# A recorder that writes the static order of a hybrid diffusion layer: another price list for TensorE, and a rule on the share of large products

## The chip, the cores and the metric

The kernel runs on one core of a Trainium2 chip. The core has five engines with queues of their own: TensorE (PE in the profile, its weight loads PEld), VectorE (DVE), ScalarE (ACT), GpSimd (POOL) and SyncE (SP, which issues the DMAs here). Each takes its instructions in the order in which the program lists them and waits on semaphores for what the others deliver. The metric is the device time of the whole kernel in microseconds, the median over runs.

## The reference, cut to what matters

Two trunk layers over 1152 tokens (128 of a prompt, 1024 of a sample), model width 1024, all in float32:

```
h      = rms_norm(x) * (1 + scale) + shift                    # adaLN
parts  = split(h @ w_in)                                      # one wide projection
o_a    = softmax(q k^T) v            * silu(gate_a)           # 8 heads, latent K and V
o_b    = b_in * conv3(c_in * x_in)   * silu(gate_b)
o_c    = rms_norm(delta_fwd(q,k,v) + delta_bwd(q,k,v)) * silu(z)
m      = s_a*(o_a @ w_pa) + s_b*(o_b @ w_pb) + s_c*(o_c @ w_pc)   # s = sigmoid(parts)
x      = x + gate * (m @ w_o)
```

`delta_*` is a gated DeltaNet in chunks of 64 tokens, 8 heads of 64 by 64, one pass forwards and one backwards. Inside a chunk a unit triangular system is solved; from chunk to chunk a state goes on, so that each chunk needs the one before:

```
v_new = u - w @ S
o     = (q*exp(g)) @ S + attn @ v_new
S     = S * exp(g_last) + k_dec^T @ v_new
```

## The kernel before

Tokens lie in three blocks of 384 columns (`CH`), features on the 128 partitions. A large float32 product is made of three products of a high and a low part (`mm3s`), each 128 by 128 by 384. The layer has three stages: the front (all of `w_in` but the merge gates, and the DeltaNet), attention, and the mix (merge gates, branch projections, output projection).

In the front the projection is one stream of work, `ip`: per tile of weights and block of tokens 24 products into one PSUM tile, which the streams `ev` and `cv` take out. Beside it run the streams of the DeltaNet, for four pairs of heads and the prompt (5 jobs): `ga` (norms `kq`, decay `sg`, Gram products `G`), `gv`, `gb` (the triangular solve of 32 by 32 blocks on DVE and POOL, 31 steps), `gz` (the products `pw` of 32 by 32 blocks), `gc` (the chain from chunk to chunk) and `gd` (the outputs `oi`, `oa`). A step of `gc` is: four calls `p` (64 by 64, into PSUM), DVE takes them out in one operation over both directions and then adds the values in two, one per direction (`scr`), four calls `pv`, DVE again, four calls `pk`, and two DVE operations, one per direction, that make the new state (`SH`). There are 16 such steps per pair of heads. A call on 64 by 64 float32 operands stands in the trace as two PE instructions: a group of four calls as x8.

The order in which every engine gets these instructions is written out while the program is built, by a list scheduler: class `Flow`. Each stream is a Python generator that yields one recorded instruction (`Op`) at a time. The front and the mix are made so; attention has an order by hand. `Flow` keeps a model clock: `free[e]` is when engine `e` is through with what it has, `ready(op)` is when the operands are there (ends of the operations that wrote them plus `LAG` between the two engines). `run` (L230) looks at the head of each stream, and takes the one that can start first, by

```
best = min(cand, key=lambda x: (x[0] + 0.02 * x[1], x[1]))
```

where x[0] is the start and x[1] the stream's rank (`RK`: gc 3; gb 6; gz, gv, gd 4; ga 7; ip 9). So a stream of rank 3 goes ahead of `ip` when it can start up to 0.12 us later. A further loop lets a lower rank in when its wait is short. `put` (L190) then moves the model's clock by the operation's cost and hands the instruction on.

The cost of a PE call comes from `Eng.cost` (L115). A product with at most 64 rows costs its number of weight columns over 600, or over 1200 where it writes to partitions other than 0: a call on 64 by 64 costs 0.107 or 0.053 us, on 32 by 32 0.053 or 0.027 us. A float32r product of 256 columns or more costs its columns over 2400 (0.160 us for 384). A float32 product of two columns (`kq`) costs 0.003 us. A DVE `tensor_tensor` costs 0.065 us and its elements over 960, `scalar_tensor_tensor` 0.131 us and the same.

All recorded instructions bear the line of the recorder that calls them (L98; those of attention and those called through other lines L95), so the rows below are told apart by the names of the tiles.

Of the kernel before, what the change touches and what calls it, by code (L numbers as in the profile page):

```python
# [39 lines left out]


class Op:
    __slots__ = ("e", "f", "r", "w", "c", "m")


class Wait:
# [9 lines left out]
def _span(ap):  # L56
    dims = ap.ap
    if ap.space == DRAM:
        lo, p0, p1 = ap.offset, 0, 1
        rest = dims  # L60
    else:
        ps, pn = dims[0]
        p0, lo = ap.offset // ps, ap.offset % ps
        p1 = p0 + pn
        rest = dims[1:]
    hi = lo + 1
    for s, n in rest:
        if s > 0:
            hi += s * (n - 1)
        else:  # L70
            lo += s * (n - 1)
    return p0, p1, lo, hi


def _free(ap):
    n = 1
    for _, k in ap.ap[1:]:
        n *= k
    return n


class Eng:
# [7 lines left out]
    def __getattr__(self, m):  # L90
        real = getattr(self.real, m)

        def call(*a, **kw):
            if not self.k.rec:
                return real(*a, **kw)  # L95
            op = Op()
            op.e = self.e
            op.f = lambda: real(*a, **kw)  # L98
            aps = [x for x in a if hasattr(x, "tensor")]
            out = kw.get("out")  # L100
            outs = [out] if out is not None else [aps.pop(0)]
            if kw.get("accum_out") is not None:
                outs.append(kw["accum_out"])
            ins = aps + [v for n, v in kw.items() if n not in ("out", "accum_out") and hasattr(v, "tensor")]
            if m == "matmul" and not kw.get("start", True):
                ins.append(outs[0])
            op.w = [(self.k.key(x), _span(x)) for x in outs]
            op.r = [(self.k.key(x), _span(x)) for x in ins]
            op.c = self.cost(m, outs[0], ins, kw)
            op.m = ins[0].ap[-1][1] / 1200.0 if self.e == "PE" else 0.0  # L110
            return op

        return call

    def cost(self, m, out, ins, kw):  # L115
        n = max([_free(out)] + [_free(x) for x in ins if x.space != DRAM]) if self.e != "PE" else _free(out)
        if self.e == "PE":
            if m == "transpose":
                return n * 2 / 2400.0
            r = ins[1].dtype == F32R  # L120
            t = n * ((1 if n >= 256 else 4) if r else 4) / 2400.0
            if ins[0].ap[0][1] <= 64:
                t = ins[0].ap[-1][1] / (1200.0 if out.offset // out.ap[0][0] else 600.0)
            return t
        if self.e == "DVE":
            return (0.131 if m == "scalar_tensor_tensor" else 0.065) + n / (160.0 if m == "reciprocal" else 960.0)
        if self.e == "ACT":
            return (0.307 if ins and ins[0].space != PSUM and n > 256 else 0.13) + n / 1600.0
        if self.e == "POOL":
            if kw.get("op") == ALU.pow:  # L130
                return 0.15 + n * 0.175
            return (0.15 if m != "tensor_tensor" else 0.1) + n / (1200.0 if m != "tensor_tensor" else 475.0)
        run = 1 << 30
        for x in [out] + ins:
            c = 1
            for st, k in reversed(x.ap[0 if x.space == DRAM else 1:]):
                if st != c:
                    break
                c *= k
            run = min(run, c)  # L140
        return out.nbytes() / 360e3 * (2 if run < 128 else 1)


class Flow:
# [8 lines left out]
    def __init__(self, k):  # L153
# [3 lines left out]
        self.ev = set()  # L157
        self.pace = {}

    def ready(self, op):  # L160
        t = 0.0
        for lst, wr in ((op.r, False), (op.w, True)):
            for key, (p0, p1, lo, hi) in lst:
                ps = key[0] == "P"
                for q0, q1, l2, h2, end, eng, w in self.log.get(key, ()):
                    if eng != op.e and ps:

                        hit = (q0 // 32 < -(-p1 // 32) and p0 // 32 < -(-q1 // 32) and l2 // 512 <= (hi - 1) // 512
                               and lo // 512 <= (h2 - 1) // 512)
                    else:  # L170
                        hit = (w or wr) and q0 < p1 and p0 < q1 and l2 < hi and lo < h2
                    if hit:
                        end += self.LAG[eng, op.e]
                        if end > t:
                            t = end
        return t

    def note(self, op, end):
        for lst, w in ((op.r, False), (op.w, True)):
            for key, sp in lst:  # L180
# [5 lines left out]
                if len(recs) > 96:  # L186
                    recs.sort(key=lambda x: x[4])
                    del recs[:32]

    def put(self, op, s):  # L190
        f = self.free
        if op.e == "SP":
            f["SP"] = s + 0.06
            hw = max(s, f.get("HW", 0.0))
            f["HW"] = hw + 0.45
            d = max(hw + 1.1, f.get("DMA", 0.0))
            f["DMA"] = d + op.c
            self.note(op, d + op.c)
        else:
            if op.e == "PE":  # L200
                s = max(s, f.get("PEW", 0.0) + op.m)
                f["PEW"] = s
            f[op.e] = s + op.c
            self.note(op, s + op.c)
        op.f()

    def step(self, st):
# [22 lines left out]
    def run(self, streams, until=None, evs=()):  # L230

        for n, s in streams.items():
            if "head" not in s:
                s.update(head=None, end=False, wait=None)
        names = sorted(streams, key=lambda n: streams[n]["rank"])
        while True:
            moved = True
            while moved:
                k0 = len(self.ev)
                for n in names:  # L240
                    self.step(streams[n])
                moved = len(self.ev) != k0
            if all(streams[n]["end"] for n in (names if until is None else until)) and all(e in self.ev for e in evs):
                return
            cand = []
            for n in names:
                op = streams[n]["head"]
                if op is not None:
                    cand.append((max(self.free.get(op.e, 0.0), self.ready(op)), streams[n]["rank"], n, op))
            if not cand:  # L250
                raise RuntimeError("streams wait for each other: %s" % {n: streams[n]["wait"] for n in names})
            best = min(cand, key=lambda x: (x[0] + 0.02 * x[1], x[1]))
            for x in cand:
                if x[3].e == best[3].e and x[1] < best[1]:
                    wait = x[0] - best[0]
                    if wait <= 0 or wait < self.WIN and wait < self.PREF * (best[3].c - wait):
                        best = x
                        break
            streams[best[2]]["head"] = None
            self.put(best[3], best[0])  # L260
# [9 lines left out]
class Kern:  # L270
# [618 lines left out]
    def conv_put(self, c, put):  # L889
        RA, RB = self.cbuf["RA"], self.cbuf["RB"]  # L890
        if c == 0:
            yield put(RA[:, 1:129], 0, 128)
            yield put(RA[:, 131:387], 128, 384)
        elif c == 1:
            yield put(RA[:, 387:580], 0, 193)
            yield put(RB[:, 0:193], 191, 384)
        else:
            yield put(RB[:, 193:577], 0, 384)
# [1652 lines left out]
```

## Time and profile before

| | |
|---|---|
| median of 3 runs | 3540.32 us (3534.69 to 3552.49) |
| the profiled execution | 3544.98 us, span 3543.2 us |
| PE busy | 3375.9 us (95%), 24654 products |
| DVE, POOL, ACT busy | 2310.6, 1538.9, 1187.1 us |
| mean granted TensorE clock | 0.97 |

By stage the span goes: front of layer 0 until about 975 us, attention until 1260, mix until 1800, then the same for layer 1 (front until 2700, attention until 2990, mix until the end). The DeltaNet's chain runs from about 300 to 850 us and from 2050 to 2590 us; these two stretches are called the mixed phases below. Busy PE means that a product is anywhere in the array: products overlap, so a time per product is best read from the start of one run of products to the start of the next.

### The profile page before, as it was taken

What the parts mean: (1) busy time and instruction counts of PE and PEld (TensorE: products, weight loads), DVE (VectorE), ACT (ScalarE), POOL (GpSimd) and SP (SyncE); (2) the same over time, 40 slices, a digit from 0 to 9 for tenths busy, and PEclk for the clock granted to TensorE, in tenths of its full rate; (3) what the DMA queues carried; (4) which work ended last, traced back from release to release, by engine and by line L of the source; (5) the groups of instructions that cost most, each with busy time, mean ns of one, the idle gap of its engine ahead of it and who ended that gap; (6) DMA issues with size and microseconds to landing.
All of it is one profiled execution on the core that took longest, in us unless ns stands there. A gap on an engine that the chain in (4) does not pass through costs nothing. (4 is left out here: it accounts for less than half of the span.)

```text
span 3543.2 us, 65525 instructions
## 1 busy us (share of the span) xinstructions
PE 3375.9 (95%) x24654; PEld 2903.7 (82%) x24654; DVE 2310.6 (65%) x5052; ACT 1187.1 (34%) x2551; POOL 1538.9 (43%) x1550
## 2 busy tenths in 40 slices
PE   7999999999899999999999999999998999999998
PEld 4988777778765699999999877777788658999998
DVE  4467776774566488856664777786455665833755
ACT  4432222223334333332444232122242443333233
POOL 3156546533157544424212645654322774444231
PEclk9999899999999999999999989999999999999999
DMA  5333213213733235466333223122256322434842
GB/s 190 98 100 77 55 54 83 59 57 122 230 83 79 51 110 162 145 203 195 123 103 107 74 75 83 47 57 73 71 187 188 73 64 70 135 100 129 256 143 87
DMA packets 381339, 389.64 MB, mean 110 GB/s; under 512 B 162016, under 2 KB 310176, under 8 KB 380640
## 3 DMA queue, kind: packets, MB, share of 16 engines
q1 hardware_dynamic: 381024, 385.46, 36.5%
q8 instruction: 195, 3.19, 0.4%
q14 instruction: 120, 0.98, 0.1%
HBM read 264.54 MB, written 120.72 MB: 109 GB/s over the span
## 5 line engine op out<-in xcount | busy, mean ns | idle before, releaser
L98 PE MATMUL ip<-h,wh_wi 128*128 128x384 f32 x5328 | 1170.5, 358 | 3.6 <-DVE gb L98 1.1
L98 PEld LDWEIGHTS ip<-h,wh_wi 128*128 128x128 f32 x5328 | 932.8, 194 | 60.1 <-issue 16.4
L95 POOL TENSOR_TENSOR acc<-acc,P 128x512 f32<-128x512 f32 x224 | 289.1, 1291 | 126.1 <-ACT P L95 110.1
L98 POOL TENSOR_TENSOR tmp<-M,X 128x2 f32<-128x2 f32 (+30 forms) x310 | 218.6, 705 | 283.4 <-DVE X L98 263.1
L95 DVE TENSOR_REDUCE mx<-s 128x1 f32<-128x384 f32 (+1 forms) x400 | 209.2, 544 | 163.9 <-PE s L95 154.5
L95 ACT ACTIVATE P<-st 128x512 f32<-128x512 f32 x292 | 173.5, 598 | 264.9 <-PE st L95 229.3
L95 PE MATMUL st<-q,K 97*128 97x512 f32 (+1 forms) x912 | 257.2, 393 | 0.0
L98 POOL TENSOR_TENSOR sl<-ss,sl 128x512 fp32r<-128x512 f32 x100 | 144.3, 1444 | 245.7 <-ACT sl L98 227.6
L98 POOL TENSOR_TENSOR wh_wi<-wri,wh_wi 128x512 fp32r<-128x512 f32 x112 | 151.9, 1366 | 155.4 <-ACT wh_wi L98 151.6
L98 PE MATMUL pp<-ob,wp 128*128 128x384 f32 x1152 | 204.1, 336 | 2.2 <-DVE ob L98 1.8
L98 DVE TENSOR_REDUCE X<-tmp 128x1 f32<-128x2 f32 (+30 forms) x620 | 184.6, 319 | 31.4 <-POOL tmp L98 23.6
L98 PEld LDWEIGHTS pp<-ob,wp 128*128 128x128 f32 x1152 | 199.1, 188 | 6.6 <-POOL ob L98 3.7
L98 PE MATMUL wop<-h,wh_wo 128*128 128x384 f32 x1152 | 202.9, 335 | 0.0
L98 PE MATMUL sg<-h,sl 128*128 128x288 f32 x1440 | 201.1, 296 | 0.1
L98 PEld LDWEIGHTS wop<-h,wh_wo 128*128 128x128 f32 x1152 | 199.7, 188 | 1.1
L98 PEld LDWEIGHTS sg<-h,sl 128*128 128x128 f32 x1440 | 194.4, 188 | 0.3 <-POOL sl L98 0.3
L98 POOL TENSOR_TENSOR mU<-mU,mt 128x384 f32<-128x384 f32 x96 | 112.6, 1173 | 182.0 <-DVE mt L98 182.0
L98 ACT ACTIVATE VT<-pv,sst 128x64 f32<-128x64 f32 x256 | 66.7, 311 | 365.4 <-DVE scr L98 349.1
L95 PEld LDWEIGHTS st<-q,K 97*128 97x128 f32 x912 | 164.0, 190 | 28.3 <-issue 11.5
L98 POOL TENSOR_TENSOR gm<-g,cst 128x256 fp32r<-128x256 f32 x144 | 107.1, 754 | 162.0 <-PE sg L98 126.3
L98 DVE TENSOR_TENSOR tmp<-M,X 128x2 f32<-128x2 f32 (+30 forms) x310 | 162.5, 524 | 18.3 <-POOL M L98 12.5
L98 DVE SCALAR_TENSOR_TENSOR ada<-wada,cs,ada 128x256 f32<-128x256 f32 x224 | 148.9, 703 | 23.2 <-DMA wada<-in_w_ada 20.7
(339 smaller groups left out, 6327.4 us busy)
## 6 DMA issues: line engine op xcount, KB each, us to landing
wri<-in_w_in SPq DMA_DIRECT2D x160, 256.0 KB, 3.4
mt<-mD SPq DMA_DIRECT2D x144, 192.0 KB, 2.9
wada<-in_w_ada SPq DMA_DIRECT2D x128, 128.0 KB, 2.3
wrp<-in_w_p SPq DMA_DIRECT2D x48, 256.0 KB, 3.6
mD<-C SPq DMA_DIRECT2D x80, 144.0 KB, 1.9
mD<-cu SPq DMA_DIRECT2D x80, 144.0 KB, 1.8
ss<-in_w_in SPq DMA_DIRECT2D x40, 256.0 KB, 4.0
ws<-in_w_in SPq DMA_DIRECT2D x40, 256.0 KB, 4.3
```

The source lines that it names most:

```text
L95: return real(*a, **kw)
L98: op.f = lambda: real(*a, **kw)
```

## The change

Only the recorder changes; each call to an engine stays as it was, and so do the operands. A PE operation gets `u` (rows, weight columns, output columns). `load` gives for it the share of the array's work (rows by weight columns over the whole array, times columns over 2400), a time (columns over 2400 plus 0.013 us from 256 columns on; 0.03 us up to 32 columns; 0.08 us for products that don't fill the array; 0.112 us else) and whether it fills the array. `product` replaces the cost in the model's clock by this time, adds 0.1 us where the product before was of the other kind, doubles it where the interval before held too little of the array's work, and keeps a list of recent products. `low` says of a small product that starts on another output than the last whether the recent work of the array, with its own, is under 0.46 of the recorder's own interval. In `run`, when the chosen operation is such a product, the first large PE product among the heads that can start within 0.1 us goes first.

```diff
@@ Eng.__getattr__: call
             op.m = ins[0].ap[-1][1] / 1200.0 if self.e == "PE" else 0.0
+            if self.e == "PE":
+                op.u = (ins[0].ap[0][1], ins[0].ap[-1][1], _free(outs[0]))
@@ Flow.__init__
+        self.win, self.part, self.last = {}, False, None
@@ Flow
+    GRID = 3.41
+    SLOW = 0.35
+    LOW = 0.46
+    SWITCH = 0.1
+    NEAR = 0.1
+    @staticmethod
+    def load(op):
+        k, m, n = op.u
+        part = k < 128 or m < 128
+        return k * m / 16384.0 * n / 2400.0, n / 2400.0 + 0.013 if n >= 256 else 0.03 if n <= 32 else 0.08 if part else 0.112, part
+    def low(self, op, s):
+        u, t, part = self.load(op)
+        if t > 0.15 or op.w[0][0] == self.last:
+            return False
+        return u + sum(x for e, x in self.recent if e > s + t - self.GRID) < self.LOW * self.GRID
+    recent = ()
+    def product(self, op, s):
+        u, t, part = self.load(op)
+        t = max(t, op.c) if t > 0.15 else t
+        if part != self.part:
+            t += self.SWITCH
+        self.part, self.last = part, op.w[0][0]
+        w = int(s / self.GRID)
+        if w > 1 and self.win.get(w - 1, 0.0) < self.SLOW * self.GRID:
+            t *= 2
+        self.win[w] = self.win.get(w, 0.0) + u
+        self.recent = [x for x in self.recent if x[0] > s - self.GRID] + [(s + t, u)]
+        return s + t
@@ Flow.put
             if op.e == "PE":
                 s = max(s, f.get("PEW", 0.0) + op.m)
                 f["PEW"] = s
-            f[op.e] = s + op.c
-            self.note(op, s + op.c)
+                f["PE"] = self.product(op, s)
+                self.note(op, f["PE"])
+            else:
+                f[op.e] = s + op.c
+                self.note(op, s + op.c)
@@ Flow.run
+            if self.LOW and best[3].e == "PE" and self.low(best[3], best[0]):
+                for x in cand:
+                    if x[3].e == "PE" and x[0] <= best[0] + self.NEAR and self.load(x[3])[1] > 0.15:
                         best = x
                         break
```

## Rows read from the trace of the kernel before

**Rows 1.** The page: its first line, and TensorE's clock in 40 slices.
```profile
span 3543.2 us, 65525 instructions
PEclk9999899999999999999999989999999999999999
```
**Rows 2.** Busy time by stretch: stretch, us, PE, PEld, DVE, ACT, POOL, clock, DMA, GB/s.
```profile
300.00:850.00 550.00, 526.76 (x5570) 414.11 (x5569) 377.02 (x1120) 139.86 (x395) 275.02 (x340) 0.93 0.26 68
2050.00:2590.00 540.00, 511.27 (x5521) 400.97 (x5520) 376.07 (x1105) 141.32 (x400) 266.00 (x336) 0.95 0.25 68
1260.00:1800.00 540.00, 527.00 (x3423) 521.46 (x3422) 397.42 (x658) 190.79 (x368) 198.48 (x153) 0.99 0.49 156
```
**Rows 3.** Groups by form, PE, first the whole span, then 300 to 850 us.
```profile
L98 PE MATMUL pp<-ob,wp 128*128 128x384 f32 x1152 | 204.1, 336 | 2.2 <-DVE ob L98 1.8
...
L98 PE MATMUL ip<-h,wh_wi 128*128 128x384 f32 x1486 | 361.6, 370 | 1.1 <-DVE gb L98 1.1
L98 PE MATMUL pv<-scr,ZT 64*64 64x64 f32 x576 | 48.5, 242 | 8.0 <-DVE scr L98 7.3
```
**Rows 4.** Timeline of PE at full clock: start, us, what, count.
```profile
501.56 0.34 PE L98 MATMUL pk<-scr,kt 64*64 64x64 f32 x8
501.84 0.79 PE L98 MATMUL ip<-h,wh_wi 128*128 128x384 f32 x3
502.60 0.30 PE L98 MATMUL p<-SH,kTb 64*64 64x64 f32 x2
...
503.46 0.38 PE L98 MATMUL sg<-gm,mr 128*128 128x256 f32 x1
...
504.86 0.30 PE L98 MATMUL pv<-scr,ZT 64*64 64x64 f32 x2
...
505.84 0.39 PE L98 MATMUL sg<-gm,mr 128*128 128x256 f32 x1
```
**Rows 5.** Timeline of PE in a stretch at half clock.
```profile
392.55 0.49 PE L98 MATMUL pk<-scr,kt 64*64 64x64 f32 x8
392.97 1.33 PE L98 MATMUL ip<-h,wh_wi 128*128 128x384 f32 x3
394.23 0.47 PE L98 MATMUL p<-SH,kTb 64*64 64x64 f32 x2
```
**Rows 6.** Busy time by stretch, as Rows 2, of that stretch.
```profile
383.00:414.00 31.00, 31.00 (x215) 22.59 (x216) 15.45 (x40) 4.53 (x15) 10.91 (x15) 0.51 0.06 20
```
**Rows 7.** Timeline of PE at full clock, groups that were not split.
```profile
519.76 0.34 PE L98 MATMUL p<-SH,kTb 64*64 64x64 f32 x8 [0.92 <-DVE SH L98]
520.04 0.62 PE L98 MATMUL ip<-h,wh_wi 128*128 128x384 f32 x2
...
521.55 0.82 PE L98 MATMUL pv<-scr,ZT 64*64 64x64 f32 x8
522.29 0.44 PE L98 MATMUL ip<-h,wh_wi 128*128 128x384 f32 x1
```
**Rows 8.** Timeline of PE: first and last pv and p split into 2 and 6.
```profile
347.24 0.47 PE L98 MATMUL pv<-scr,ZT 64*64 64x64 f32 x2
...
358.35 0.30 PE L98 MATMUL p<-SH,kTb 64*64 64x64 f32 x2
...
2466.71 0.47 PE L98 MATMUL p<-SH,kTb 64*64 64x64 f32 x2
...
2517.09 0.32 PE L98 MATMUL pv<-scr,ZT 64*64 64x64 f32 x2
```
**Rows 9.** Timeline of PE: products with two columns.
```profile
491.18 3.57 PE L98 MATMUL kq<-hm,P 128*128 128x2 f32 x16
```
**Rows 10.** Timeline of PE: first and last place where groups of two tiles stand together.
```profile
369.70 0.32 PE L98 MATMUL G<-kqT 64*64 64x128 f32 x1
...
2515.34 0.27 PE L98 MATMUL oa<-VT,at 64*64 64x64 f32 x2
```
**Rows 11.** Groups by form, DVE, 300 to 850 us.
```profile
L98 DVE TENSOR_TENSOR scr<-scr,vT 64x128 f32<-64x128 f32 x128 | 53.6, 419 | 3.6
L98 DVE SCALAR_TENSOR_TENSOR SH<-SH,egl,pk 128x64 f32<-128x64 f32 x112 | 26.4, 277 | 16.5 <-PE pk L98 16.0
L98 DVE TENSOR_TENSOR scr<-p,sst 128x128 f32<-128x128 f32 x64 | 18.3, 286 | 13.5 <-PE p L98 13.5
```
**Rows 12.** Groups by form, PE, 842 to 890 us, then 2573 to 2645 us.
```profile
L98 PE MATMUL ip<-h,wh_wi 128*128 128x384 f32 x176 | 34.5, 342 | 0.0
...
L98 PE MATMUL ip<-h,wh_wi 128*128 128x384 f32 x249 | 48.3, 341 | 0.0
```

More of the change, by code (lines that the diff above doesn't have):

```diff
@@ L42 @@
 class Op:
-    __slots__ = ("e", "f", "r", "w", "c", "m")
+    __slots__ = ("e", "f", "r", "w", "c", "m", "u")
 class Wait:
@@ L256, in run @@
                     if wait <= 0 or wait < self.WIN and wait < self.PREF * (best[3].c - wait):
+                        best = x
+                        break
+            if self.LOW and best[3].e == "PE" and self.low(best[3], best[0]):
+                for x in cand:
+                    if x[3].e == "PE" and x[0] <= best[0] + self.NEAR and self.load(x[3])[1] > 0.15:
                         best = x
```

## The prediction

> **What bounds the kernel now.** The page comes first: a span of 3543.2 us, and a TensorE clock that is full nearly everywhere [rows 1]. The dips lie in the two mixed phases, so the busy time by stretch is next: in 300 to 850 us PE is busy for 526.8 of 550 us at a mean clock of 0.93, in 2050 to 2590 us for 511.3 of 540 at 0.95, and the next engine, DVE, for 377 and 376 [rows 2]. PE bounds these phases, with 23 and 29 us idle. Since the clock has two levels, 1.2 and 2.4 GHz, the means say how long it stood at the lower: 2 x 0.07 x 550 + 2 x 0.05 x 540 = 131 us. The reader is to see a second loss too: 1486 `ip` products take 361.6 us in the first phase, 0.243 each, while the same shape in a dense stage takes 204.1 / 1152 = 0.177 [rows 3]. The timeline shows why. Groups of small products stand between runs of `ip`, and a group with its way in and out is dear: `pk` x8 and three `ip` take from 501.56 to 502.60, 1.04 us, of which 3 x 0.177 = 0.53 are `ip`; the group costs 0.51 [rows 4]. So PE's time is `ip` + groups x (their work + a change of kind) + what the half clock adds + idle time. The change can touch the last three.
>
> **How good the two price lists are.** For that sequence the old list gives 2 x 0.107 + 2 x 0.053 + 3 x 0.160 = 0.80 us, the new one 0.1 + 4 x 0.08 + 0.1 + 3 x 0.173 = 1.04. The row says 1.04 [rows 4]. With the old list PE comes 0.24 us late at the next group; with the new one it comes on time. That is the root of both a gain and a loss below.
>
> **Clock.** The same sequence at the lower clock takes from 392.55 to 394.23, 1.68 us [rows 5]. So (1.68 - 1.04) / 1.68 = 0.38 of the time at half clock is lost, 0.38 x 131 = 50 us; that is the upper end. In the longest of these stretches the clock is 0.51 although PE is busy for 31.00 of 31 us [rows 6]; what it does there is single `ip` among small groups, and the rule in `low` puts more `ip` there. The Trainium skill, "TensorE: Matmul & The Clock Gate" (What's actually happening), has the clock follow how busy PE has been and fall after an idle window. The row stands against the second half of that, as PE had no idle time; by the page the rule could return nothing here, which is a rival below. The recorder counts columns and rows, not busy time, and where its prices are right it keeps `ip` in. They are wrong for `kq`: x16, eight calls, took 3.57 us at half clock [rows 9], and the new list says 8 x 0.03 = 0.24. It will not see these stretches, and it can't break into a group that writes one tile. I take 0.7 of the 50: 35 us. Lower end: a loss of 15, if the `ip` now used leaves other stretches bare (0.38 x some 40 us).
>
> **Split groups.** 54 `pv` and 24 `p` groups stand as x2, some `ip`, x6; the first and last are in [rows 8]. In the model the reason is plain: the first of four calls ends after 0.053 or 0.107 us, but its partner waits for a second DVE operation of 0.065 + 128/960 = 0.2 us. The wait left is 0.147 or 0.093, the handicap of `ip` 0.12: about every other group lets an `ip` in. The new list charges 0.1 + 0.08 for the first call, the wait left is 0.02, and the group stays whole, unless `ip` was the better choice for another reason. Price: a split `p` takes from 502.60 to 503.46, less one `ip` 0.68 [rows 4]; a whole one from 519.76 to 520.04, 0.28 [rows 7]: 0.40 saved. A split `pv` takes 0.98 - 0.177 = 0.80 [rows 4], a whole one that waits inside 0.74 [rows 7], one that doesn't 0.28 like `p`: 0.06 to 0.52, and I take 0.22, nearer the row of the same tile, since the DVE operation is as late either way. Sum 24 x 0.40 + 54 x 0.22 = 21.5 us, ends 13 and 38; three quarters of it, 16. Should other groups be cut instead (a `pw` waits 0.6 us in the model for its DVE transposes), it may be a loss of 5.
>
> **Seams opened.** In 63 places groups of two or three tiles stand together without an `ip`, with 86 seams [rows 10]. There the rule will push `ip` in between when its share is low. A seam opened costs one more way in and out, 0.51 - 0.28 = 0.23 us [rows 4, 7]. Ends: 86 x 0.23 = 20 us, and a gain of 10 where more groups become ready together because PE's clock runs slower in the model; I take a third of the worse end, 7.
>
> **Cover that goes.** DVE is slower than its price: an addition of the values takes 0.419 us for 0.198, the operation before it 0.286 for 0.198, one of the new state's 0.277 for 0.198 [rows 11]. A step holds two, one and two of them: 0.44 + 0.09 + 0.16 = 0.69 us late. Today PE is late by about three times 0.24 = 0.72, so it finds the data there. With the right prices for PE alone that cover is gone, and behind a waiting `pv` stand all `ip`, for the queue is in order; the streams `ev` and `w` wait for these. Upper end 0.69 x 128 steps = 88 us. Against it: where `low` strikes, a group comes later than it could; groups like `oi` are still dearer than 0.52; half of DVE's lateness lies where other groups stand between. Lower end: a gain of the 8 us per phase that PE now waits before `pv` [rows 3]. I take 12, nearer to these waits than to the 88.
>
> **At nothing:** start and mix. Prices for 384 columns go from 0.160 to 0.173, for 288 from 0.120 to 0.133; the order between DVE, ACT and POOL may shift, but in the mix PE is busy for 527 of 540 us [rows 2], and its operands are ahead. If that cover fails somewhere, the 13 us idle there grow by a few. Attention's order is by hand. No DMA is added; those of `w` keep their place in their stream.
>
> **Sum.** 3545.0 (the profiled execution) - 35 - 16 + 7 + 12 = 3513. That execution lies 4.7 us above the median of the runs, so against that median 3508.
>
> **Rivals.** (a) Everything comes back and nothing is paid: 3545 - 50 - 22 - 5 = 3468. For it speaks that the new price met the row to 0.01; against it `kq` and DVE. (b) More `ip` among the groups doesn't hold the clock: PE is without a gap in the 31 us at half clock [rows 6], and filling what has no gap returns nothing. Then 3545 - 16 + 7 + 12 - 5 = 3543, no change. Against it: these dips lie where groups stand between the `ip`, and the dense stage has a clock of 0.99 [rows 2]. This is the outcome by the rule of the Trainium skill named above. (c) DVE becomes the wait: half of the 88 us instead of 12, 3508 + 32 = 3540, no change. For it speak [rows 11]; against it, the old order has few waits of this sort. (d) Slower: `ip` runs out. After the DeltaNet's last product 176 and 249 `ip` remain [rows 12], 425 x 0.177 = 75 us, and they fill PE while norms and second projections wait on DVE. If `low` draws them all ahead, the chain of the DeltaNet grows by what they take, and the stretch behind has no filling: up to 75 us idle; with 65 of it, 3508 + 65 = 3573. It decides from the point where some 50 of the 75 are lost, two thirds; against it speaks that a plain step meets the rule already: three groups at 0.52 and twelve `ip` at 0.173 are 3.6 us, of which 12 x 0.160 = 1.9 us count, over 0.46.
>
> **How the numbers follow.** Forecast 0.45, (a) 0.13, (b) 0.12, (c) 0.12, (d) 0.18. Within 0.5%, 18 us, can't be told from no change: 3523 to 3558. The forecast's own range is 3485 to 3530; some four fifths of it are faster, with (a) and a little of the rest 0.52. Slower: (d), and what (c) and (b) leave on that side, 0.22. Same: 0.26. The range goes from a part of (a) to the middle of (d): 3450 to 3575.
>
> **What would show it.** Right: a clock near 0.98 in both phases, with `kq` under the dips that remain; hardly any `p` or `pv` as x2 and x6; `pk` x8 with `ip` as before. (c) would show as waits of PE before `pv` well over the 8 us of the first phase [rows 3]; (d) as no `ip` after the last `ot` and PE idle under the norms. Wrong from the ground: equal dips at more `ip`, or as many splits as before.

## The result and the profile after

The changed kernel takes 3667.15 us (median of 4 runs, 3657.0 to 3672.17), the kernel before 3546.4 us beside it (4 runs): a ratio of 1.0353, 95% interval [1.0321, 1.0385]. It is slower by 3.5%, where 3508 us was forecast and 3575 was the upper end. The profiled execution of after took 3657.0 us.

The page of after, first line and clock, against [rows 1]: the clock, nearly full throughout before, now dips oftener and deeper in the mixed phases (slices 4 to 8, and 24 to 27).

```profile
span 3655.2 us, 65546 instructions
PEclk9997879799999999999999988989999999999999
```

Busy time by stretch, columns as in [rows 2]; first the kernel before over exactly its two mixed phases (first `pw` to last `ot`), then after over its own.

```profile
320.00:842.00 522.00, 499.85 (x5418) 387.77 (x5417) 362.65 (x1084) 135.07 (x385) 263.33 (x323) 0.93 0.23 64
2052.00:2573.00 521.00, 494.22 (x5421) 384.91 (x5420) 368.96 (x1089) 134.59 (x384) 260.09 (x327) 0.94 0.24 65
```
```profile
319.00:901.00 582.00, 528.57 (x5413) 406.15 (x5413) 372.15 (x1094) 133.99 (x384) 261.86 (x326) 0.86 0.21 57
2100.00:2636.00 536.00, 489.06 (x5325) 375.19 (x5325) 370.05 (x1097) 129.83 (x377) 254.34 (x324) 0.91 0.21 58
1300.00:1613.00 313.00, 291.70 (x2047) 286.71 (x2046) 238.96 (x404) 110.39 (x230) 126.83 (x85) 0.97 0.40 126
503.00:513.00 10.00, 10.00 (x61) 7.23 (x61) 6.56 (x19) 1.10 (x4) 2.48 (x2) 0.50 0.67 231
```

The first phase holds the same number of PE instructions within five and takes 60 us longer. PE is idle in it for 53 us (582 - 528.6), before for 22. The clock has gone from 0.93 to 0.86. The third line of after is the first part of the mix (below), the fourth a stretch at half clock.

PE groups of the first mixed phase, before and then after (busy, mean ns, idle ahead and who ended it):

```profile
L98 PE MATMUL ip<-h,wh_wi 128*128 128x384 f32 x1334 | 335.0, 374 | 0.0
L98 PE MATMUL pv<-scr,ZT 64*64 64x64 f32 x576 | 48.5, 242 | 8.0 <-DVE scr L98 7.3
L98 PE MATMUL p<-SH,kTb 64*64 64x64 f32 x480 | 28.2, 251 | 4.2 <-DVE SH L98 3.6 <-DVE X L98 0.3
```
```profile
L98 PE MATMUL ip<-h,wh_wi 128*128 128x384 f32 x1329 | 354.8, 397 | 0.0
L98 PE MATMUL pv<-scr,ZT 64*64 64x64 f32 x576 | 45.0, 253 | 19.0 <-DVE scr L98 17.8 <-ACT YA L98 0.6
L98 PE MATMUL p<-SH,kTb 64*64 64x64 f32 x480 | 23.3, 266 | 9.1 <-DVE SH L98 7.3
L98 PE MATMUL pw<-ZT,P 32*32 32x32 f32 x576 | 15.3, 209 | 11.6 <-DVE ZT L98 9.3 <-ACT ZT L98 2.4
```

The wait before `pv`, small in [rows 3], has more than doubled; that before `p` has doubled, and that of `pw` for VectorE has grown from 0.2 to 9.3 us. In the second phase the waits before `pv` and `p` grew less, first before and then after (us in total, times, longest):

```profile
PE pv L98 <- DVE scr L98: 10.0, 23, 1.1
PE p L98 <- DVE SH L98: 6.2, 12, 1.4
```
```profile
PE pv L98 <- DVE scr L98: 18.1, 28, 1.9
PE p L98 <- DVE SH L98: 8.1, 16, 1.4
```

So of the idle time that came, these two waits have 24 us over both phases; the rest stands before `pw`, `ot`, `oi` and others.

VectorE's operations of the chain are no slower than in [rows 11] by more than 6 ns; what grew is VectorE's own wait for PE (28.3 us ahead of `scr<-p`, 13.5 before). The two engines wait for each other:

```profile
L98 DVE TENSOR_TENSOR scr<-scr,vT 64x128 f32<-64x128 f32 x128 | 54.2, 423 | 3.7
L98 DVE SCALAR_TENSOR_TENSOR SH<-SH,egl,pk 128x64 f32<-128x64 f32 x112 | 26.7, 283 | 25.8 <-PE pk L98 25.6
L98 DVE TENSOR_TENSOR scr<-p,sst 128x128 f32<-128x128 f32 x64 | 18.4, 288 | 28.3 <-PE p L98 28.1
```

The timeline of PE in after, in place of [rows 4, 5, 7, 8]: the groups are whole, and yet all this runs at half clock (from 500.4 to 514.0 us).

```profile
501.04 1.00 PE L98 MATMUL pv<-scr,ZT 64*64 64x64 f32 x8 [0.95 <-DVE scr L98]
501.97 1.65 PE L98 MATMUL ip<-h,wh_wi 128*128 128x384 f32 x4
503.55 0.49 PE L98 MATMUL pk<-scr,kt 64*64 64x64 f32 x8
503.97 1.01 PE L98 MATMUL ip<-h,wh_wi 128*128 128x384 f32 x2
504.91 0.49 PE L98 MATMUL p<-SH,kTb 64*64 64x64 f32 x8
505.33 1.97 PE L98 MATMUL ip<-h,wh_wi 128*128 128x384 f32 x5
```

Behind the last `ot`, 228 and 496 `ip` are left (176 and 249 in [rows 12]): they did not run out.

```profile
L98 PE MATMUL ip<-h,wh_wi 128*128 128x384 f32 x228 | 44.6, 343 | 0.0
...
L98 PE MATMUL ip<-h,wh_wi 128*128 128x384 f32 x496 | 95.4, 338 | 0.0
```

**One account for all kernels.** From a trace I count over both mixed phases: their length; how long the clock stood at half and how often it fell; PE's idle time; the changes of kind, between products that fill the array (128 by 128) and products that don't; and the `ip` themselves. Length less 0.177 us for each `ip` [rows 3], less 0.38 of the half clock [rows 4, 5], less idle leaves a rest:

```
                        ratio  length  falls  half  idle  changes    ip  ip/us  rest
before                  1       1043    14    130    49    1276   2669  2.56   472
after                   1.035   1118    24    263   100    1188   2566  2.30   463
x1_prices_only          1.094   1277    22    809   160     870   2249  1.76   412
x2_rule_only            1.007   1048    12     96    41    1304   2810  2.68   473
x3_chain_dear           1.032   1122    21    150    89    1250   2842  2.53   472
m1_mix_old              1.029   1134    34    280   104    1168   2626  2.32   459
p_all_te_dearer         1.054   1117    28    346   119    1144   2260  2.02   467
h_no_switch_price       1.019   1084    20    198    79    1170   2671  2.46   457
h_floor_higher          1.030   1148    26    191    87    1164   2964  2.58   463
z_level_back            1.004   1032    13    106    65    1164   2660  2.58   456
q_all_engines_dearer    1.029   1148    13    195    65    1310   2960  2.58   486
q_others_cheaper        1.020   1026    25    205    96    1050   2260  2.20   452
h_hold_groups           0.993    988    11     82    58    1108   2590  2.62   441
w_hold_cheaper          0.988    988    12     68    49    1100   2693  2.73   436
w_hold_wider            0.993    973    18    116    68    1048   2430  2.50   430
w_hold_and_rule         0.999   1032    20    154    55    1182   2631  2.55   453
```

The rest goes with the changes: a straight line through the 16 rows has 0.16 us for each change, and the rows lie within 13 us of it. So the account closes to about that much. The price of half clock can be seen apart from it, in executions of one and the same order: 23 of the kernel before have clocks from 0.964 to 0.977 and times from 3553 to 3519 us, and the time goes up by 0.38 us with each us of half clock. This also says how far a single row can be trusted. The rows are one execution each, and 0.013 of the clock is 2 x 0.013 x 3540 = 92 us of half clock over the span, so a difference of some 50 us in `half` between two rows shows nothing by itself; that of before and after, 133 us, is larger, and all executions of after lie at 0.946 to 0.952. From before to after: half clock 133 us more, times 0.38 = +50; idle +51; rest -9. The mix adds 34 us (first part, `mg` and `sg`, +15.3 and +11.6 by layer; `pp` +4.4 and +2.3). All other stages, their `ip` at 0.177 taken out, are 13 shorter. Sum 113; the spans differ by 112.0.

### The profile page after: what moved, and what is told of

It reads as the page before. It is cut to its first block, busy times and chain, and to the rows that moved or that the text cites. A ratio compares the mean times of both kernels' runs of the same rounds, so it can differ in the third digit from the quotient of the medians.

```text
span 3655.2 us, 65546 instructions
## 1 busy us (share of the span) xinstructions
PE 3424.1 (94%) x24654; PEld 2933.4 (80%) x24654; DVE 2301.5 (63%) x5052; ACT 1189.2 (33%) x2551; POOL 1539.4 (42%) x1550
## 5 line engine op out<-in xcount | busy, mean ns | idle before, releaser
L98 PE MATMUL ip<-h,wh_wi 128*128 128x384 f32 x5328 | 1205.2, 366 | 4.2 <-DVE h L98 3.2
L98 PEld LDWEIGHTS ip<-h,wh_wi 128*128 128x128 f32 x5328 | 956.7, 200 | 62.3 <-issue 19.8
L98 ACT ACTIVATE wh_wi<-wri 128x512 fp32r<-128x512 f32 x156 | 95.9, 627 | 176.8 <-DMA wri<-in_w_in 90.1
```

## The experiments

Theory A: the old prices were too low on every engine, and their ratio was near right; the new list makes TensorE alone dearer, the recorder takes it for the scarce engine, and the order that suits such a chip waits and loses the clock on this one. Theory B: the rule or the shape of the prices (by tile size, by change of kind) does it.

**Prices without the rule**, and **the rule without the prices** (both from after):

```diff
# x1_prices_only
-    LOW = 0.46
+    LOW = 0
# x2_rule_only, in product: old cost, no price of a change, no doubling
-        t = max(t, op.c) if t > 0.15 else t
-        if part != self.part:
-            t += self.SWITCH
+        t = op.c
...
-        if w > 1 and self.win.get(w - 1, 0.0) < self.SLOW * self.GRID:
-            t *= 2
```

> The changed kernel with the rule on the share off (LOW = 0): the new prices alone. Theory A (cover): with TensorE priced right and DVE still too low, TensorE arrives before DVE's data; the prices do the harm, the rule only softens it. Then both mixed phases keep more than 100 us of idle TensorE together (49 before the change, 100 after it), the half-clock time there stays above 260 us (130 before, 263 after), and the whole takes 3640 to 3720 us. Theory B (rule): the rule holds ready groups back and so delays the DeltaNet's chain; without it the time comes back to 3560 us or less. The mix stage, where the rule finds nothing to do, stays as after the change by both (sg stages 313 and 295 us).

> The old prices with the rule on the share (no change of kind, no doubling, old cost per product). Theory A: the old prices keep their cover, idle TensorE in the two mixed phases stays at 40 to 65 us (49 before), the mix stays as before (sg stages 298 and 283 us); the rule only moves some ip forward; 3520 to 3570 us, within 1% of before. Theory B: the rule does the harm; 3620 us or more, with idle TensorE and half clock as after the change.

x1: 3871.52 us, ratio 1.0944 [1.0925, 1.0964]; x2: 3557.93 us, 1.0065 [1.004, 1.0091]. The new list does the harm, not the rule; without the rule it was worse than expected (3640 to 3720 us). One part of the list explains that: where the interval before held too little of the array's work, `product` doubles the price. In x1's order 1802 and 2029 of the 3231 and 3232 products of the mixed phases were doubled, in after's 104 and 21. So x1 isn't after less the rule at the same prices: in the books the rule's main effect is to keep the doubling off. Busy time of x1 in its first mixed phase: PE is idle for 81 of 632 us, and the clock is 0.69.

```profile
323.00:955.00 632.00, 551.22 (x5210) 422.47 (x5209) 378.83 (x1093) 128.28 (x371) 249.21 (x321) 0.69 0.18 48
```

x2 comes out as theory A has it. Its rule does put more `ip` among the groups (2.68 a us). The row has 34 us less half clock, but that is no gain shown: over the whole span its five executions stand at clocks of 0.965 to 0.971, and the kernel before beside them at 0.970 to 0.976. It also has only 75 `ip` left for the first second projection.

**The chain's work dearer in the front** (from after), and **old prices in the mix** (from after):

```diff
# x3_chain_dear, in step; the front sets fl.chain = 1.45
+                if self.chain and st["rank"] in (3,) and x.e in ("DVE", "ACT"):
+                    x.c *= self.chain
# m1_mix_old, in put; the mix sets fl.old = True
-                f["PE"] = self.product(op, s)
+                f["PE"] = s + op.c if self.old else self.product(op, s)
# m1_mix_old, in run: no rule in the mix either
-            if self.LOW and best[3].e == "PE" and self.low(best[3], best[0]):
+            if self.LOW and not self.old and best[3].e == "PE" and self.low(best[3], best[0]):
```

> The changed kernel, and DVE and ACT instructions of the stream gc alone (the chain from chunk to chunk) are charged 1.45 times in the front, which brings them near what the trace shows. Theory A: the cover comes back from the other side: idle TensorE in the mixed phases under 70 us (100 after the change), half clock there under 200 us (263), 3580 to 3620 us; the mix stays as after the change. Theory B, or one in which the prices of TensorE themselves are wrong: no better than after the change, 3640 to 3690 us.

> The changed kernel, but in the mix (until the next front begins) the old prices and no rule. Theory A holds for the mix as well (288 columns at 0.133 instead of 0.120 us take TensorE's cover away, and it waits for DVE's ada and POOL's sl): the sg stages come back from 313 and 295 us to 298 and 283, the pp stages from 170 and 168 to 166, the whole to 3625 to 3645 us. If these stages differ for another reason (they start from another order in the fronts), they stay, and the whole stays at 3655 to 3670 us.

x3: 3653.48 us, 1.0317 [1.0286, 1.0349]: a miss for theory A, whose sign was idle under 70 us and 3580 to 3620 us; the time lies where the expectation put its rival (3640 to 3690). Idle stayed at 89. Half clock is at 150 us in the row, but that execution, 3635.04 us at a clock of 0.962, is the best of four (the others 0.956 and 0.957). So pricing right only the one chain that I had seen late is not enough, and its lateness is not shown to be what PE waits for in after. (The edit goes by rank and makes `lb`, behind the phases, dearer too.) m1: 3639.98 us, 1.029 [1.0262, 1.0317], as expected: the mix's loss is the new price (0.133 for 0.120 us at 288 columns). m1 takes out price and rule together, but x1, which has no rule, keeps the loss: its first part of the mix is 15 and 12 us longer than before's. What PE waits for in the first part of the mix, after and then m1:

```profile
PE adc L98 <- DVE ada L98: 10.9, 6, 7.1
PE sg L98 <- POOL sl L98: 7.0, 10, 2.0
```
```profile
PE adc L98 <- DVE ada L98: 5.0, 1, 5.0
PE sg L98 <- POOL sl L98: 4.3, 3, 2.2
```

Six waits for VectorE in place of one, ten for GpSimd in place of three: an order made with PE 11% dearer and the others as they were. The front of m1 stays as bad as after's (table).

**TensorE dearer, nothing else** (from before; the front's old PE prices times 1.25):

```diff
-        fl.pace = {}
+        fl.pace = dict(PE=1.25)
```

> The kernel before with one edit: in the forward stages every old TensorE price times 1.25; no price by the tile's size, no price for a change of kind, no rule. Theory A (it is the level of TensorE's price against the other engines' that does the harm: TensorE looks scarce, so the small groups that are ready go first and fewer products of the input projection lie between them): the clock falls more often as with the prices alone, half clock in the two mixed phases well over 250 us (130 before), a time of 3650 to 3800 us, ratio 1.03 to 1.07. Rival B (it is the prices by tile size, which make the 64-row tiles cheap beside the full ones, or the price of a change of kind): all prices rise alike here, so nothing changes in their order of worth, and the time is within 1% of before, 3505 to 3575 us. The static order leaves about 10% fewer input products in the mixed phases than before (1147 and 1111 against 1333 and 1336).

3724.57 us, 1.0543 [1.0497, 1.0589]. A dearer TensorE is enough for the harm: no rule, no price of a change, no price by size, and the loss is all there and more, with after's marks: 28 falls, 119 us idle, 2.02 `ip` a us.

```profile
308.00:883.00 575.00, 516.23 (x5237) 396.88 (x5236) 379.05 (x1100) 129.32 (x374) 252.77 (x323) 0.82 0.20 53
2135.00:2678.00 543.00, 483.15 (x5197) 366.94 (x5196) 366.37 (x1092) 127.84 (x371) 250.70 (x322) 0.87 0.21 55
```

**Parts of the new list** (from after): no price of a change; a higher floor; the whole list back at the old level, its shape, its price of a change (which the edit also divides by 1.3, to 0.077 us, other than its expectation says) and the rule kept.

```diff
# h_no_switch_price
-    SWITCH = 0.1
+    SWITCH = 0.0
# h_floor_higher
-    LOW = 0.46
+    LOW = 0.52
# z_level_back, in product
-        t = max(t, op.c) if t > 0.15 else t
+        t = op.c if t > 0.15 else t / 1.3
         if part != self.part:
-            t += self.SWITCH
+            t += self.SWITCH / 1.3
```

> The changed kernel without the 0.1 us price of a change between whole and part tiles; the other prices, the doubling and the rule stay. Theory A: the dear TensorE is still there (a 64-row group keeps its prices), so most of the loss stays: 3600 to 3680 us, ratio 1.015 to 1.04, idle of TensorE in the two mixed phases about 80 to 110 us. Rival B: it is the 0.1 us that holds the groups together and drives the joins apart, and without it the time falls to 3545 to 3590 us, with the splits back at 35 in place of 9 a layer (16 of p and 19 of pv in the static order).

> The changed kernel with the floor of the rule at 0.52 in place of 0.46: the static order then puts 1481 input products into each mixed phase (1327 and 1239 after, 1333 and 1336 before). If half clock comes from too few input products an interval on the chip, half clock falls from 263 us back to 130 us or less, which at 0.38 us each is 50 us; the idle of TensorE (100 us, 49 before) is another matter in theory A (work on VectorE and ScalarE late against a TensorE order that was packed by too low prices) and stays; each input product more costs 0.177 us in this phase and saves the same later, but the second projection of the first layer has 73 input products left for 175 before, and pays some 10 us for that. Sum: 3600 to 3640 us, ratio 1.017 to 1.03. If the rule itself does harm (by moving input products in front of small ones that the chain waits for), idle rises and the time is 3670 or more.

> The changed kernel with its TensorE prices taken back to the old level and nothing else: full products at their old price, small ones at the new price divided by 1.3; the price by tile size, the 0.1 us of a change of kind, the doubling and the rule stay. The 2107 small products of a mixed phase then cost the recorder 141 us (147 before, 181 after), the static order has 1362 and 1296 input products in the mixed phases. Theory A (the level of TensorE's prices against the other engines' does the harm): 3530 to 3590 us, ratio 0.997 to 1.013, half clock below 180 us in the two mixed phases. Rival B (the shape of the new prices, the 0.1 us or the rule do it): 3620 to 3680 us, ratio 1.02 to 1.04. It should not come below the kernel with the groups held, which has the groups whole without a dear TensorE.

No price of a change: 3602.65 us, 1.0188 [1.0145, 1.0231]. Higher floor: 3642.32 us, 1.0302 [1.0259, 1.0345]; half clock fell by 72 us, not by 133, and more `ip` in the phases paid little. Level back: 3550.12 us, 1.0044 [1.0025, 1.0064]. With the same shape and rule but the old level, nearly all of the loss is gone, that of the mix with it: half clock 106, 13 falls.

```profile
331.00:850.00 519.00, 485.42 (x5452) 378.83 (x5451) 365.52 (x1089) 136.09 (x388) 261.32 (x325) 0.96 0.24 65
2051.00:2565.00 514.00, 482.87 (x5385) 375.51 (x5384) 367.38 (x1080) 133.54 (x381) 258.03 (x322) 0.94 0.23 64
```

In the recorder's own books the 2107 products of a mixed phase that are not `ip` cost 147 us before, 181 after, 182 with TensorE times 1.25, 146 without the price of a change, 141 with the level back. The last two agree in the books (phases of 412 and 405 us against 410 and 396), but not on the chip: without the price of a change the phases take 52 us longer (198 us of half clock against 106), and the mix keeps its dear 288 columns. So the level of TensorE's prices is what most of the loss hangs on, and what the shape of the list adds stays open.

**Ratio or level** (both from before):

```diff
# q_all_engines_dearer
+        fl.pace = dict(PE=1.25, DVE=1.25, ACT=1.25, POOL=1.25)
# q_others_cheaper
+        fl.pace = dict(DVE=0.8, ACT=0.8, POOL=0.8)
```

> The kernel before with the prices of TensorE, VectorE, ScalarE and GpSimd in the forward stages all times 1.25 (transfers as before). With TensorE's alone times 1.25 the time was 1.054 of before. If it is the ratio of TensorE's price to the others' that does the harm, that is gone: 3520 to 3575 us, ratio 0.995 to 1.01, half clock in the two mixed phases below 180 us, 46 and 217 input products left for the second projections (10 us more in the first of them). If it is the level itself (against the recorder's fixed numbers in us and the prices of transfers), 3650 us or more, ratio above 1.03.

> The kernel before with the forward prices of VectorE, ScalarE and GpSimd times 0.8 and TensorE's left as they are: the same ratio as TensorE's times 1.25, at the old level of TensorE. If the ratio decides, the loss is the same as with TensorE dearer: 3650 to 3760 us, ratio 1.03 to 1.06, half clock above 250 us in the two mixed phases. If TensorE's level decides, 3520 to 3575 us, ratio 0.995 to 1.01. The splits of p and pv fall from 133 to 63 in the static order, worth some 10 us either way.

3645.05 us, 1.0292 [1.0266, 1.0317], and 3614.94 us, 1.0201 [1.0176, 1.0226]. Neither theory had it whole; the square is nearly additive. The ratio costs 2.0% (1.0201 to 1) or 2.4% (1.0543 to 1.0292), the level 2.9% or 3.4%. The table tells which of them is at work in the change. Ratio alone gives after's picture (25 falls, 96 us idle, 2.20 `ip` a us). Level alone gives another one (13 falls, 65 us idle, 2.58 `ip` a us; it loses by 291 more `ip` in the mixed phases, 52 us, of which the projections ahead and behind give back 17, and by one stretch of 78.5 us at half clock). So outside the mixed phases, with `ip` at 0.177 taken out, the level costs 35 us or more, where after, apart from its mix, is 13 us shorter. First the two phases of q_others_cheaper, then of q_all_engines_dearer:

```profile
309.00:824.00 515.00, 470.13 (x5224) 363.70 (x5223) 366.00 (x1092) 130.34 (x375) 250.79 (x319) 0.89 0.22 58
2060.00:2570.00 510.00, 459.29 (x5198) 354.79 (x5197) 363.27 (x1095) 126.88 (x371) 252.36 (x321) 0.91 0.22 58
```
```profile
319.00:880.00 561.00, 530.89 (x5609) 415.11 (x5608) 366.94 (x1111) 140.11 (x396) 272.48 (x344) 0.95 0.23 65
2077.00:2665.00 588.00, 553.49 (x5562) 430.40 (x5560) 367.63 (x1101) 137.62 (x392) 268.90 (x337) 0.88 0.22 61
```

By these marks it is the ratio in the front; that is an argument from likeness, as no run gives the change's own list the old ratio at its new level. The change makes small products 1.23 times as dear, near to the 1.25 of the square; 2.0 to 2.4% with the mix's 0.6% (m1 against after) would be 2.6 to 3.0 of the 3.5%. By which of the recorder's fixed numbers a common level works stays open.

**Whole groups without a price.** The splits can be had directly (from before): when a small product of a group has gone out, the next of the same output goes first if it can start soon.

```diff
# h_hold_groups, in run; put sets self.last = op.w[0][0] for PE
+            if best[3].e == "PE":
+                for x in cand:
+                    if x[3].e == "PE" and x[3].w[0][0] == self.last and x[0] <= best[0] + 0.2 and x[3].c < 0.12:
+                        best = x
+                        break
# w_hold_cheaper adds fl.pace = dict(PE=0.95); w_hold_wider has 0.5 for 0.2
# w_hold_and_rule is x2_rule_only with this and LOW = 0.40
```

> The kernel before with its old prices and one new preference: after a small product of a group, the next product of the same output tile goes first if it can start within 0.2 us of the best. No price and no rule of the change. Splits fall to 5 for the two layers' p and pv together, changes of kind from 639 and 637 to 555 and 553 a mixed phase. If a split costs the 0.2 us that the prediction read from its rows, 130 splits fewer are worth 15 to 25 us: 3513 to 3523 us, ratio 0.993 to 0.996. If a group's whole time counts less (the splits of the changed kernel gave back only 8 us), 3530 us, ratio 0.997 to 1.0. If small groups that are kept whole push the input products apart and the clock falls more often, 3545 to 3580 us.

> The kernel with the groups held, and every old TensorE price of the forward stages times 0.95. If a dearer TensorE does harm because the price's level sets the order (theory A), a cheaper one need not gain: the old ratio of prices was about right. The static order puts 110 and 55 more input products ahead of the mixed phase, and 59 and 187 are left for the second projections (178 and 335 with the groups held alone). Expected 3490 to 3530 us; if the second projection of the first layer runs out of input products, up to 20 us more in it, 3520 to 3540 us. A ratio of 0.985 to 1.0 to the kernel before.

> The kernel with the groups held, where the next product of the group may start up to 0.5 us after the best candidate in place of 0.2. Changes of kind fall from 555 and 553 to 525 and 523 a mixed phase, the tiles of pw that are cut from 53 to 38 a layer, and input products in the mixed phases from 1331 and 1259 to 1216 and 1212. A change of kind costs about 0.2 us, 60 of them are worth 12 us; waits of up to 0.5 us for a group's next product, some 40 a layer, cost as much, and with fewer input products between the groups the clock may fall more often, as with the dear TensorE. Expected 3500 to 3550 us, ratio 0.99 to 1.003; below 0.99 if the wait is hidden.

> The kernel with the groups held, with the rule of the change at a floor of 0.40 and old prices. The rule alone took 10 us off each mixed phase and gave them back in a second projection that had fewer input products; here 148 and 324 are left for the second projections, near to the 178 and 335 without the rule. If the half clock that is left (82 us in the two mixed phases, 31 us of time at 0.38 each) falls by a third, 3495 to 3510 us, ratio 0.988 to 0.992; the changes of kind rise again from 555 to 595 and from 553 to 587, which at 0.2 us costs 15 us, and then it is no better than the groups held alone: 3505 to 3525 us, ratio 0.99 to 0.997.

Held groups: 3509.77 us, 0.9925 [0.99, 0.995], a little better than expected. The account, from one execution that took 3503.75 us: 168 changes fewer, rest -31, so 0.18 us each; half clock 48 us less, -18; idle +9. PE waits more for `scr` than before (15.3 us in the first phase, 7.3 before) and yet the kernel is faster: a wait that holds a group together is paid for by the change of kind that it saves.

```profile
318.00:815.00 497.00, 469.98 (x5413) 372.08 (x5412) 373.42 (x1084) 134.91 (x385) 260.19 (x323) 0.96 0.24 66
2024.00:2515.00 491.00, 460.52 (x5348) 362.36 (x5347) 363.53 (x1079) 132.78 (x380) 254.67 (x321) 0.96 0.25 67
```
```profile
PE pv L98 <- DVE scr L98: 15.3, 32, 1.5
```

With TensorE 5% cheaper: 3496.39 us, 0.988 [0.9854, 0.9906], the best of all, and once more in the direction of A, though its interval and that of the held groups meet. Held wider: 3513.52 us, 0.9929 [0.9901, 0.9956], no better. With the rule: 3535.51 us, 0.9988 [0.9969, 1.0008], a miss; half clock was to fall, and rose from 82 to 154 us in the rows (the row is the second slowest of 12 executions; by the median clocks, 0.974 and 0.9675, the rise is some 45 us). The rule lets `ip` in ahead of a group that the clock didn't need it for, and raises the changes by 74; why the clock falls more often then, I can't say.

## Why the prediction was wrong

**Clock** (-35) has the wrong sign: +50. Its premise was that the rule puts more `ip` among the groups. On the chip there are fewer, 2.56 a us before and 2.30 after. By itself the rule does put more in (x2: 2.68); the prices took out more than it put in, and the step looked at the rule alone. The rule also counts in the recorder's time. There the mixed phases held 3.44 `ip` a us before and hold 2.87 and 2.82 after; the chip takes 1.26 and 1.22 times as long, so a floor kept in the books is not kept on the chip. The step also read [rows 6] too closely. PE is busy there, but the row of before just ahead of the fall at 383.4 us has a wait:

```profile
382.22 0.39 PE L98 MATMUL sg<-gm,mr 128*128 128x256 f32 x1 [1.22 <-POOL gm L98]
```

That is how most falls look: the waits that end in the 6 us ahead of each of the 24 falls of after come to 1.51 us on average, where 6 us of the phases hold 0.54. So a wait goes with a fall, and may cost itself and what the clock takes behind it; no run here takes the waits away alone. The price of half clock, 0.38, was right, as the 23 executions above show. The Trainium skill, "TensorE: Matmul & The Clock Gate" (What's actually happening), has the clock fall after idling and rise with a busy PE. On the fall the trace agrees better than the prediction granted, in so far as waits go before it, though PE was busy for 5.72 of the 7 us ahead of the fall at 383.4; on the rise it doesn't: from 503 to 513 us PE is busy for 10.00 of 10 us at a clock of 0.50. Rival (b), that filling returns nothing, was not tried as such, since the filling did not come in after; but x2, with 2.68 `ip` a us, shows no higher clock than before, and the higher floor, with 2.58, has 191 us of half clock where before, with 2.56, has 130. More `ip` a us is not enough to keep the clock.

**Split groups** (-16): the mechanism was right. Cut `p` and `pv` fell from 133 to 18 in the order. A group split by an `ip` has two changes of kind more, at 0.18 by the held groups 0.36 us, so the 0.22 to 0.40 for one was about right too. But 115 splits fewer would be up to 230 changes, and only 88 went: changes came in elsewhere. **Seams** (+7) was the term for such changes; the two together were put at -9, and the rest fell by 9. With rows that lie up to 13 us off the line this may be luck.

**Cover that goes** (+12) named the mechanism and its bound (88), and chose too near to the waits of before: idle +51. The waits before `pv` and `p`, which were its mechanism, have 24 of the 51; the waits before `pw`, `ot` and others were in no term, and x3, with the chain's operations dearer, did not take the idle time away. What failed is the choice by the nearest row: waits of the old order measure how well that order fits, and say nothing on a new one. I saw that DVE's prices were 1.4 to 2.1 times too low [rows 11] and PE's 1.3 times [rows 4], and then counted it a gain to right one of them. Rival (c) put half of the 88, 44 us, on this; the idle time came near that size, half of it by (c)'s wait, and the clock came on top.

**At nothing: the mix** is +34, from the dearer 288 columns. The prediction had "its operands are ahead" from PE's busy time; they were not ahead of an order in which PE alone had become dearer. **Rival (d)** is out. A rule that draws `ip` forward was the wrong fear; the dear PE left more of them behind.

## What to carry to other kernels

The prices of a list scheduler like this one work by their ratio between engines and against its fixed numbers (handicaps, lags): making one engine's prices true, while the others stay too low, gave an order with more waits and less clock, and cost 3.5%. Before a difference of clock between two kernels is explained, look at how far it differs between executions of one. Want a property of the order (a group kept whole)? State it as a rule of choice, which gained 0.75%, and not as a price. A floor that a model keeps in its own time must be read off the chip's trace.

## What the runs showed of the hardware

A change between products that fill the array and products of 64 or 32 rows has a price of its own, 0.15 to 0.18 us: 0.18 by the held groups, (472 - 412) / 406 = 0.15 by x1 (with half clock at 0.38), 0.16 by the line through all 16 kernels. The Trainium skill, "TensorEngine Tiling (Array Packing)" (Key Properties), says that a switch of tiling mode drains the engine; no run here tells what the drain has of this price.

PE can be busy without a gap and stay at the lower clock. From 503 to 513 us of after PE has no idle time and stays at 0.50, and the kernel before does so for 31.00 us at 0.51 [rows 6], while from 500 to 507 us of before a sequence like it runs without a gap at a clock of 1.00 [rows 4]. One thing that differs is what went before. Ahead of the fall at 500.4 us in after stands a wait for GpSimd, and across it the wait of 0.95 us for `scr` shown above (timeline of PE in after):

```profile
499.43 0.66 PE L98 MATMUL ot<-cst,on 128*128 128x128 f32 x4 [1.65 <-POOL on L98]
```

The clock rises at 514.0 us, with PE as busy as before; what brought it back is open.
